# The beginning of a hybrid decoder step: tokens in halves, the first weight block loaded ahead of x, identity products on TensorE

## The chip, the core and the metric

The kernel runs on one core of one Trainium2 chip. The metric is the device time of one execution in microseconds, and a version's time is the median of its runs. In the profile PE is TensorE's products, PEld its weight loads, DVE the vector engine, ACT the scalar engine, POOL GpSimd, and SP the engine that issues most DMAs. A name with a q behind it (ACTq, SPq) is the engine's queue issuing a DMA.

## The reference, cut to what matters

One layer of a decoder trunk. All three head groups (NSA attention, RWKV-7, memory attention) read the same projection of the normalised tokens, 1024 of the prompt and 8 samples:

```python
h = rms_norm(x_prompt, ln_g)                 # x_prompt: 1 x 1024 x 1024
q, kv, g, z, u_rw, z_rw, q_mem, z_mem = split_in(h @ w_in)    # w_in: 1024 x 3480
# the same for x_sample (8 x 1 x 1024)
prev = concatenate([prev_row, u_rw[:-1]]); u = u_rw + (prev - u_rw) * mu
# then the recurrence on u, two kinds of attention, gates and the output projection
```

Only the start of this is touched by the change: the normalisation, h and the first columns of the projection, u_rw (896 columns from column 1816 on).

## The kernel before, in words

The prompt's 1024 tokens are worked in two halves H of 512 tokens, four tiles of 128 tokens each. For a product of near full precision each operand is split in a high part, rounded to fp32r, and a low part, the rest: three products (high x high, high x low, low x high) stand for one.

`load_x` (L171) loads four tiles x of 128 x 1024. `norm_x` (L180) squares each on ACT with a running sum (L186), makes the reciprocal root by nine small operations on DVE for each tile (`rsqrt`, L118: L125 to L136), and scales the tile in place on DVE (L188). `load_xs` does the same for the samples. `make_hTs` (L222) turns the samples' rows on TensorE (p_hs, L228), multiplies by the gains on DVE (hs, L231), and POOL writes the high and low parts into the last eight columns of each h tile (L235, L236). `make_hT` (L202) turns x on TensorE: for each of eight blocks k of 128 channels four transposes fill one PSUM tile p_h (L208); ACT writes the high part of h, 128 x 512 (L211), and DVE the low part (L212).

`w_load` (L241) loads a block of 128 columns of w_in on SP (wraw, two buffers), and `w_split` (L250) makes its high part on ACT (whi, L255) and its low part on DVE (wlo, L256), two buffers each. `project` (L259) multiplies one block with one half of the tokens: for H = 0 in two pieces of 256 and 264 columns, p_pr (L268), 24 products each; three PSUM tiles are there for p_pr. `u_half` (L530) runs over the seven blocks of u_rw, and `do_u` (L285) mixes each with the row before it on ACT (L294) and DVE (L301 to L307).

The order of the program: samples, four x tiles, two weight blocks, the other four x tiles (all these loads on SP but the samples' one), norm of the first half, hs, split of the two blocks, h of the first half, block 0 with its two pieces interleaved by k, blocks 1 to 6; the norm of the second half and its h are woven into these. A scheduler puts each engine's instructions into one fixed order from this; every engine works strictly in that order. `issue_after` holds a group back until an instruction named in it is placed. `rwkv_open` (L575) loads constants from ACT's queue.

Of the kernel before, what the change touches and what calls it, by code (L numbers as in the profile page):

```python
# [10 lines left out]
F32 = mybir.dt.float32  # L11
# [3 lines left out]
AF = mybir.ActivationFunctionType  # L15
OP = mybir.AluOpType
# [3 lines left out]
D = 1024  # L20
T = 1024
NS = 8
HALF = 512
# [24 lines left out]
def bc(ap, shape):  # L48
    return ap.to_broadcast(shape)
# [18 lines left out]
def group(gen, n):  # L68

    while list(islice(gen, n)):  # L70
        yield
# [42 lines left out]
class Step:  # L114
# [53 lines left out]
        return self.vec[:, k:k + n]  # L168


    def load_x(self, H):  # L171
        xs = []
        for t in range(4):
            x = self.xp.tile([128, D], F32, name="x", tag="x", bufs=8)
            r0 = H * HALF + t * 128
            self.nc.sync.dma_start(x[:], self.I["x_prompt"][0, r0:r0 + 128, :])
            xs.append(x)
        return xs

    def norm_x(self, xs):  # L180
        nc = self.nc
        self.xn = {}
        ss = self.small.tile([128, 4], F32, name="ss_x")
        for t in range(4):
            j = self.xp.tile([128, D], BF, name="sqx", tag="sqx", bufs=1)
            self.last_sq = nc.scalar.activation(j[:], xs[t][:], AF.Square, accum_out=ss[:, t:t + 1])  # L186
            r = self.rsqrt(self.small, ss[:, t:t + 1], 1, 1.0 / D, 1e-6)
            self.last_x = nc.vector.tensor_scalar(xs[t][:], xs[t][:], r, None, op0=OP.mult)  # L188
            self.xn[t] = xs[t]

    def load_xs(self):
        nc, I = self.nc, self.I
        x = self.xp.tile([128, D], F32, name="xs", tag="xs")
# [5 lines left out]
        nc.vector.tensor_scalar(x[:NS], x[:NS], r, None, op0=OP.mult)  # L199
        self.xsn = x  # L200

    def make_hT(self, H):  # L202

        nc = self.nc
        for k in range(8):
            ps = self.pw.tile([128, 512], F32, name="p_h", tag="w") if k % 2 and H == 0 else self.ptr.tile([128, 512], F32, name="p_h", tag="tr")
            for t in range(4):
                nc.tensor.transpose(ps[:, t * 128:(t + 1) * 128], self.xn[t][:, k * 128:(k + 1) * 128], self.ident[:])  # L208
            hi, lo = (x[k] for x in self.h8) if H == 0 else self.h_tiles(H, k)
            g = self.v("ln_g", k)  # L210
            nc.scalar.activation(hi[:, :HALF], ps[:], AF.Copy, scale=g)  # L211
            nc.vector.scalar_tensor_tensor(lo[:, :HALF], ps[:], g, hi[:, :HALF].bitcast(F32),  # L212
                                           op0=OP.mult, op1=OP.subtract)
            self.hi[H].append(hi)
            self.lo[H].append(lo)
            yield

    def h_tiles(self, H, k):
        W = HALF + (NS if H == 0 else 0)
# [1 line left out]

    def make_hTs(self):  # L222
        nc = self.nc
        self.h8 = list(zip(*(self.h_tiles(0, k) for k in range(8))))
        if True:
            ps = self.ptr.tile([128, 512], F32, name="p_hs", tag="tr")
            for k in range(8):
                nc.tensor.transpose(ps[:, k * NS:(k + 1) * NS], self.xsn[:NS, k * 128:(k + 1) * 128],  # L228
                                    self.ident[:NS, :NS])
# [17 lines left out]
        self.last_w = nc.sync.dma_start(raw[:, :, :n], src)  # L247
        return raw

    def w_split(self, raw, n):  # L250
# [4 lines left out]
        nc.scalar.activation(hi[:, :, :n], raw[:, :, :n], AF.Copy)  # L255
        nc.vector.tensor_tensor(lo[:, :, :n], raw[:, :, :n], hi[:, :, :n].bitcast(F32), op=OP.subtract)  # L256
        return hi, lo

    def project(self, H, hi, lo, m, out, first=False):  # L259

        pieces = ((0, 256), (256, 520)) if H == 0 else ((0, 512),)
        pss = [self.ppr.tile([128, 512], F32, name="p_pr", tag="pr") for _ in pieces]
        parts = [(ps, a, b, k) for ps, (a, b) in zip(pss, pieces) for k in range(8)]
        if first:
            parts.sort(key=lambda x: x[3])
        for n, (ps, a, b, k) in enumerate(parts):
            for i, (w, h) in enumerate(((hi, self.hi[H]), (hi, self.lo[H]), (lo, self.hi[H]))):
                self.last_mm = self.pe.matmul(ps[:m, :b - a], w[:, k, :m], h[k][:, a:b],  # L268
                                              start=(k == 0 and i == 0), stop=(k == 7 and i == 2))
# [143 lines left out]
    def phase1(self):  # L413
        tc, nc, I, O = self.tc, self.nc, self.I, self.O
# [7 lines left out]
        with ExitStack() as ctx:  # L422
# [18 lines left out]
            self.pe = self.te = nc.tensor  # L441
            with ExitStack() as xctx:
                self.xp = xctx.enter_context(tc.tile_pool(name="xp", bufs=1, reuse_waits="tile"))
                self.load_xs()
# [84 lines left out]

    def u_half(self, H):  # L530
        self.U = self.up.tile([128, 2, 7, 256], F32, name="U")
        for j in range(7):
            hi, lo = self.ready.pop(0) if self.ready else self.wblock(1816 + j * 128, 128)
            out = []
            yield from self.project(H, hi, lo, 128, out, (H, j) == (0, 0))
            self.do_u(H, out, j)

    def columns(self, tiles):
# [902 lines left out]
    def phase2(self):  # L1441
        tc, nc, I, O = self.tc, self.nc, self.I, self.O
        with ExitStack() as ctx:
# [23 lines left out]
            ready, spent = [0.0] * 4, [0.0] * 4  # L1467
            rate = START

# [363 lines left out]
    def sample_nsa(self):  # L1833
# [3 lines left out]
        with ExitStack() as ctx:  # L1837
# [15 lines left out]
            with P("snsx") as xp:  # L1853
# [479 lines left out]
```

## Time and profile before

| | |
|---|---|
| runs | 1008.6, 1008.91, 1014.28 us; median 1008.91 |
| the profiled execution | 1011.9 us |
| its span, first to last instruction | 1010.1 us, mean granted clock 0.981 |
| busy | PE 948.4 (94%), PEld 788.3 (78%), DVE 679.4 (67%), ACT 441.9 (44%), POOL 252.1 (25%) |
| PE in the first of 40 slices (25 us) | 5 tenths; 9 or more in 33 of the others, 8 or less in 6 |

The shares are means over stages of different kinds. For an edit at the start one reads the start: the timeline of the first microseconds, engine by engine, and, in square brackets, how long the engine sat idle before a row and what released it. A row of the timeline merges neighbours of one kind; the number behind the x says how many.

### The profile page before, as it was taken

Reading aid. Unit: us, or ns where it says so; the run is one execution under the profiler, and the core shown is the slowest. Engines: PE = TensorE matmul, PEld = TensorE weight load, DVE = VectorE, ACT = ScalarE, POOL = GpSimd, SP = SyncE. Lnnn points to the kernel's source line nnn. Section 1 sums busy time; section 2 is a strip of 40 time slices with the busy share of each in tenths; the row PEclk is TensorE's granted clock in tenths of the full one; section 3 lists DMA queues with packets and bytes.
Section 4 is the critical chain, followed back from the end, with each engine's and each line's share of the span. In section 5 each row is a group of like instructions: output and inputs, shape, how many; then the busy total and the mean of one; then the engine's idle time right before and its main releaser. Section 6 shows DMA issues by size and latency. Waiting matters only on the chain.

```text
span 1010.1 us, 24649 instructions
## 1 busy us (share of the span) xinstructions
PE 948.4 (94%) x9887; PEld 788.3 (78%) x9887; DVE 679.4 (67%) x1965; ACT 441.9 (44%) x987; POOL 252.1 (25%) x220
## 2 busy tenths in 40 slices
PE   5999999999999998999987999999999988999997
PEld 4999888778887877788866777887878876777964
DVE  7669489546773997543547677775779986457465
ACT  7554333223532432223425666656467655224312
POOL 1000000000000000000007765766578853112010
PEclk9999999899999999999996999999999999999999
DMA  8323114113230162256245323331210063995522
GB/s 280 105 64 89 41 53 116 54 44 85 72 106 3 50 176 65 59 135 156 66 148 177 101 64 100 132 87 39 50 38 17 27 148 100 297 290 185 153 78 76
DMA packets 133979, 104.20 MB, mean 103 GB/s; under 512 B 34594, under 2 KB 121129, under 8 KB 133737
## 3 DMA queue, kind: packets, MB, share of 16 engines
q1 hardware_dynamic: 128904, 90.92, 31.3%
q0 software_dynamic: 3200, 10.49, 3.1%
q8 instruction: 78, 1.28, 0.5%
q10 hardware_dynamic: 1760, 1.21, 0.4%
q14 instruction: 37, 0.30, 0.1%
HBM read 84.00 MB, written 22.78 MB: 106 GB/s over the span
## 4 chain that ended last, share of the span: by engine, by line
PE 35%; DVE 10%; ACT 6%; DMA 3%; issue 2%; SPq 2%; POOL 1%; ACTq 0%; DVEq 0%; POOLq 0%
PE p_s L86 5%; PE p_pT L86 5%; PE p_out L86 5%; PE p_pr L268 4%; PE p_o L86 4%; PE p_pr L86 2%; ACT p L1298 2%; DMA wor<-in_w_out_dram 2%; ACT p L1307 1%; PE p_hid L86 1%; DVE nm L1297 1%; PE p_sc L86 1%; SPq L1818 1%; DVE pt L1258 1%; POOL p L1312 1%
## 5 line engine op out<-in xcount | busy, mean ns | idle before, releaser
L86 PE MATMUL p_pr<-h,whi 128*128 128x512 f32 (+5 forms) x928 | 234.2, 344 | 2.3 <-issue 2.3
L1312 POOL TENSOR_SCALAR p<-p,fac 128x640 f32<-128x640 f32 (+7 forms) x128 | 211.2, 1665 | 93.8 <-DVE fac L1309 37.4
L86 PEld LDWEIGHTS p_pr<-h,whi 128*128 128x128 f32 (+1 forms) x928 | 149.3, 186 | 21.8 <-issue 5.3
L86 PE MATMUL p_pr<-h,wlo 128*128 128x512 f32 (+5 forms) x464 | 154.3, 332 | 0.0
L959 POOL MEMSET w2d<- 128x128 f32 x1 | 0.2, 205 | 388.5 <-PE p_it L86 388.5
L86 PEld LDWEIGHTS p_pr<-h,wlo 128*128 128x128 f32 (+1 forms) x464 | 86.3, 186 | 9.9
L268 PE MATMUL p_pr<-h,whi 128*128 128x256 f32 (+2 forms) x416 | 87.2, 306 | 0.4 <-ACT whi L255 0.2
L86 PE MATMUL p_pT<-ident,p 128*128 128x128 f32 x528 | 74.4, 285 | 5.1 <-ACT pt L1256 2.3
L86 PE MATMUL p_s<-kh,qs 128*128 128x512 f32 (+3 forms) x191 | 72.3, 386 | 4.5 <-ACT p L1298 4.5
L86 PEld LDWEIGHTS p_pT<-ident,p 128*128 128x128 f32 x528 | 58.7, 144 | 17.4 <-issue 7.1
L86 PE MATMUL p_o<-pt,vs 128*64 128x128 f32 x1056 | 70.0, 282 | 1.1 <-DVE c_r L1232 0.7
L1298 ACT ACTIVATE p<-p_s,nm 128x640 f32<-128x640 f32 (+3 forms) x64 | 55.7, 873 | 33.4 <-DVE nm L1297 27.5
L1297 DVE TENSOR_REDUCE nm<-p_s 128x1 f32<-128x640 f32 (+3 forms) x64 | 57.6, 918 | 17.4 <-PE p_s L86 17.3
L268 PEld LDWEIGHTS p_pr<-h,whi 128*128 128x128 f32 x416 | 66.3, 190 | 3.7 <-ACT whi L255 0.7
L256 DVE TENSOR_TENSOR wlo<-wraw,whi 128x1024 fp32r<-128x1024 f32 (+1 forms) x35 | 41.8, 1196 | 37.3 <-ACT whi L255 37.3
L86 PEld LDWEIGHTS p_o<-pt,vs 128*64 128x64 f32 x1056 | 59.0, 140 | 6.7 <-issue 2.7
L268 PE MATMUL p_pr<-h,wlo 128*128 128x256 f32 (+2 forms) x208 | 62.7, 303 | 0.2 <-DVE wlo L256 0.2
L86 PE MATMUL p_s<-kl,qs 128*128 128x512 f32 (+3 forms) x192 | 62.6, 342 | 0.0
L1258 DVE COPY pt<-p_pT 128x512 f32<-128x512 f32 (+1 forms) x72 | 48.0, 671 | 17.2 <-PE p_pT L86 16.7
L255 ACT ACTIVATE whi<-wraw 128x1024 fp32r<-128x1024 f32 (+1 forms) x35 | 36.3, 1038 | 51.5 <-PE p_pr L86 37.8
L1256 ACT ACTIVATE pt<-p_pT 128x512 f32<-128x512 f32 (+1 forms) x72 | 42.1, 588 | 30.6 <-PE p_pT L86 30.1
L86 PE MATMUL p_out<-woh,chi 128*128 128x512 f32 x128 | 52.3, 408 | 1.7 <-ACT woh L2154 1.6
(535 smaller groups left out, 1985.8 us busy)
## 6 DMA issues: line engine op xcount, KB each, us to landing
wraw<-in_w_in_dram SPq DMA_DIRECT2D x34, 512.0 KB
pg<-in_c_pool_dram SPq DMA_DIRECT2D x40, 256.0 KB
pg<-in_c_pool_dram SPq DMA_DIRECT2D x48, 128.0 KB
x<-in_x_prompt_dram SPq DMA_DIRECT2D x8, 512.0 KB
z_d<-zt SPq DMA_DIRECT2D x16, 256.0 KB
cat<-z_d SPq DMA_DIRECT2D x8, 512.0 KB
xres<-in_x_prompt_dram POOLq DMA_DIRECT2D x16, 256.0 KB, 3.9
wor<-in_w_out_dram SPq DMA_DIRECT2D x16, 256.0 KB
```

The lines of the kernel that those rows point to most:

```text
L86: self.last = getattr(self.engine, op)(*a, **k)
L255: nc.scalar.activation(hi[:, :, :n], raw[:, :, :n], AF.Copy)
L256: nc.vector.tensor_tensor(lo[:, :, :n], raw[:, :, :n], hi[:, :, :n].bitcast(F32), op=OP.subtract)
L268: self.last_mm = self.pe.matmul(ps[:m, :b - a], w[:, k, :m], h[k][:, a:b], start=(k == 0 and i == 0), stop=(k == 7 and i == 2))
L959: nc.gpsimd.memset(w2d[:], 0.0)
L1256: nc.scalar.activation(pt[:, :n], ps[:, :n], AF.Copy)
L1258: nc.vector.tensor_copy(pt[:, :n], ps[:, :n])
L1297: V.tensor_reduce(nm[:, h, b:b + 1], ps[:, c0:n1], axis=AX.X, op=OP.max, negate=True)
L1298: A.activation(Ps[h, b][:, :n1 - c0], ps[:, c0:n1], AF.Exp, bias=nm[:, h, b:b + 1], accum_out=sm[:, h, b:b + 1])
L1307: A.activation(Ps[h, b][:, :n1], ps[:, h, :n1], AF.Exp, bias=nm[:, h, b:b + 1], accum_out=sm[:, h, b:b + 1])
L1312: nc.gpsimd.tensor_scalar(x, x, f[:, h, b:b + 1], None, op0=OP.mult)
L1818: self.last_page = nc.sync.dma_start(dst[:, c], page[:, c0:c0 + 256])
```

## The change

Seven edits, all in the first phase:

- SP loads weight block 0 ahead of the four x tiles and block 1 behind them; ACT and DVE split block 0 before the first row sums.
- The norm goes by two tiles at a time: one reciprocal root of two columns in twelve steps for both. In the later two of four tiles, the last one's scale is done by ACT and no longer by DVE.
- h goes by halves of 256 tokens: a PSUM tile p_h now holds two k of 256 columns. ACT's and DVE's operations on it have 256 columns and are twice as many.
- Blocks 0 and 1 both do their first 256 tokens before either does its last 264.
- Block 1's low part is made on POOL.
- 34 products of the identity with itself (p_w, plain f32) stand first on TensorE; nothing reads them.
- The four squares of the second half's tiles are held until the last high part of the first half is placed.

The diff's core:

```diff
+WARM = 34
-    def norm_x(self, xs):
-        ss = self.small.tile([128, 4], F32, name="ss_x")
-        for t in range(4):
-            self.last_sq = nc.scalar.activation(j[:], xs[t][:], AF.Square, accum_out=ss[:, t:t + 1])
-            r = self.rsqrt(self.small, ss[:, t:t + 1], 1, 1.0 / D, 1e-6)
-            self.last_x = nc.vector.tensor_scalar(xs[t][:], xs[t][:], r, None, op0=OP.mult)
+    def square_x(self, xs):
+        ss = self.small.tile([128, 2], F32, name="ss_x")
+        for t, x in enumerate(xs):
+            self.last_sq = nc.scalar.activation(j[:], x[:], AF.Square, accum_out=ss[:, t:t + 1])
+        return ss
+    def norm_x(self, xs, t0, ss=None):
+        ss = ss or self.square_x(xs)
+        r = self.rsqrt(self.small, ss[:], 2, 1.0 / D, 1e-6)
+        for t, x in enumerate(xs):
+            if t and t0:
+                nc.scalar.activation(x[:], x[:], AF.Copy, scale=r[:, t:t + 1])
+            else:
+                self.last_x = nc.vector.tensor_scalar(x[:], x[:], r[:, t:t + 1], None, op0=OP.mult)
+    def warm(self):
+        ps = self.pw.tile([128, 512], F32, name="p_w", tag="w")
+        for n in range(WARM):
+            self.nc.tensor.matmul(ps[:, :128], self.ident[:], self.ident[:], start=True, stop=True)
...
+    def make_hT(self, H, half):
+        for k0 in range(0, 8, 2):
+            pool, tag = (self.pw, "w") if k0 % 4 and H == 0 else (self.ptr, "tr")
+            ps = pool.tile([128, 2, 256], F32, name="p_h", tag=tag)
+            for j in range(2):
+                for t in range(2):
+                    nc.tensor.transpose(ps[:, j, t * 128:(t + 1) * 128],
+                                        self.xn[2 * half + t][:, (k0 + j) * 128:(k0 + j + 1) * 128], self.ident[:])
+            for j in range(2):
...
+                self.last_hi = nc.scalar.activation(hi[:, c], ps[:, j], AF.Copy, scale=g)
+                self.last_lo = nc.vector.scalar_tensor_tensor(lo[:, c], ps[:, j], g, hi[:, c].bitcast(F32),
+                                                              op0=OP.mult, op1=OP.subtract)
...
-                self.load_xs()
-                xs0 = self.load_x(0)
-                raws = [self.w_load(1816 + j * 128, 128) for j in range(2)]
-                xs1 = self.load_x(1)
-                self.norm_x(xs0)
-                self.make_hTs()
-                with tc.issue_after(self.last_x.ins):
-                    self.ready = [self.w_split(raw, 128) for raw in raws]
-                for _ in self.make_hT(0):
-                    pass
+                self.warm()
+                self.load_xs()
+                raws = [self.w_load(1816, 128)]
+                xs0 = self.load_x(0, range(4))
+                raws.append(self.w_load(1816 + 128, 128))
+                xs1 = self.load_x(1, range(4))
+                self.ready = [self.w_split(raws[0], 128)]
+                self.norm_x(xs0[:2], 0)
+                scaled = self.last_x.ins
+                self.norm_x(xs0[2:], 2)
+                self.ready.append(self.w_split(raws[1], 128, G))
+                with tc.issue_after(scaled):
+                    self.make_hTs()
+                first = self.u_half(0)
+                with tc.issue_after(self.last_sq.ins):
+                    for half in range(2):
+                        for _ in self.make_hT(0, half):
+                            pass
+                        for _ in range(4):
+                            next(first)
                 with tc.issue_after(self.last_sq.ins):
                     self.rwkv_open()
-                first = self.u_half(0)
-                for _ in range(8):
+                for _ in range(16):
                     next(first)
-                self.norm_x(xs1)
-                for _ in weave(group(first, 8), self.make_hT(1)):
+                with tc.issue_after(self.last_hi.ins):
+                    sss = [self.square_x(xs1[t:t + 2]) for t in (0, 2)]
+                for t in (0, 2):
+                    self.norm_x(xs1[t:t + 2], t, sss[t // 2])
+                for _ in weave(group(first, 8), chain(self.make_hT(1, 0), self.make_hT(1, 1))):
                     pass
...
     def u_half(self, H):
+        begun = [[], []] if H == 0 else []
+        for pieces in ((0, 256),), ((256, 520),):
+            for j, out in enumerate(begun):
+                hi, lo = self.ready[j]
+                for n, _ in enumerate(self.project(H, hi, lo, 128, out, pieces)):
+                    yield
+                if len(out) == 2:
+                    self.do_u(H, out, j)
```

What this does to the fixed orders is not plain from the diff. In the rows below a row of the new program has the line numbers of the new file. First TensorE from its first product on; p_hs are the samples' transposes, p_h those of x, p_pr the projection. Before:

```order
L228 MATMUL p_hs<-ident,xs 128x8 x8
L208 MATMUL p_h<-ident,x 128x128 x20
L268 MATMUL p_pr<-h_0_219,whi 128x256
L268 MATMUL p_pr<-h_0_219,whi 128x264
L268 MATMUL p_pr<-h_0_219,whi 128x256
L208 MATMUL p_h<-ident,x 128x128 x4
L268 MATMUL p_pr<-h_0_220,whi 128x256
L268 MATMUL p_pr<-h_0_219,wlo 128x256
```

And in the change:

```order
L203 MATMUL p_w<-ident 128x128 x34
L246 MATMUL p_hs<-ident,xs 128x8 x8
L223 MATMUL p_h<-ident,x 128x128 x16
L284 MATMUL p_pr<-h_0_243,whi 128x256 x2
L284 MATMUL p_pr<-h_0_244,whi 128x256
L284 MATMUL p_pr<-h_0_243,wlo 128x256
L284 MATMUL p_pr<-h_0_244,whi 128x256
L284 MATMUL p_pr<-h_1_245,whi 128x256
L223 MATMUL p_h<-ident,x 128x128 x4
L284 MATMUL p_pr<-h_1_246,whi 128x256
```

The 34 products stand ahead of everything, the samples' transposes too. The 16 transposes are those of the first two x tiles; the next four, of the other two tiles, stand between products of k = 0 and k = 1. From about the 410th row on TensorE's order is the same in both programs.

Second, ACT from the samples' square on. Before:

```order
L197 ACTIVATE sqx,ss_s<-xs 8x1024
L186 ACTIVATE sqx,ss_x<-x 128x1024 x4
L255 ACTIVATE whi<-wraw 128x1024 x2
L579 DMA c_rw<-in_c_rw_dram 128x480
L586 DMA wa_328<-in_rwkv_w_dram 64x256
L587 DMA wa_328<-in_rwkv_a_dram 64x256
L601 DMA lnw<-in_rwkv_ln_w_dram 128x256
L601 DMA lnw<-in_rwkv_ln_b_dram 128x256
L211 ACTIVATE h_0_219<-p_h,vec 128x512
```

And in the change:

```order
L211 ACTIVATE sqx,ss_s<-xs 8x1024
L273 ACTIVATE whi<-wraw 128x1024
L186 ACTIVATE sqx,ss_x<-x 128x1024 x4
L619 DMA c_rw<-in_c_rw_dram 128x480
L273 ACTIVATE whi<-wraw 128x1024
L626 DMA wa_411<-in_rwkv_w_dram 64x256
L232 ACTIVATE h_0_243<-p_h,vec 128x256
```

Block 0's split has come to the front; block 1's still stands ahead of the first part of h, and three of the five DMA issues have gone behind that part.

Third, ACT again, a little later: the last parts of h of the first 256 tokens, the issues, and a part of the next 256 tokens (h_7 to h_3).

```order
L232 ACTIVATE h_7_257<-p_h,vec 128x256
L627 DMA wa_411<-in_rwkv_a_dram 64x256
L641 DMA lnw<-in_rwkv_ln_w_dram 128x256
L641 DMA lnw<-in_rwkv_ln_b_dram 128x256
L232 ACTIVATE h_3_249<-p_h,vec 128x256
```

The three issues stand between the two halves of the first half's h. Seven rows on, behind the last part of h of the next 256 tokens, the change has the later squares:

```order
L232 ACTIVATE h_7_257<-p_h,vec 128x256
L186 ACTIVATE sqx,ss_x<-x 128x1024
L659 ACTIVATE rk<-U,vec 128x256
L310 ACTIVATE U<-p_pr,dv 128x256
L186 ACTIVATE sqx,ss_x<-x 128x1024
L659 ACTIVATE rk<-U,vec 128x256
L186 ACTIVATE sqx,ss_x<-x 128x1024
L310 ACTIVATE U<-p_pr,dv 128x256
L273 ACTIVATE whi<-wraw 128x1024
```

Before, the same place reads so:

```order
L211 ACTIVATE h_5_229<-p_h,vec 128x512
L186 ACTIVATE sqx,ss_x<-x 128x1024
L211 ACTIVATE h_4_227<-p_h,vec 128x512
L211 ACTIVATE h_7_233<-p_h,vec 128x512
L211 ACTIVATE h_6_231<-p_h,vec 128x512
L186 ACTIVATE sqx,ss_x<-x 128x1024 x3
L159 DMA gains<-in_nsa_q_norm_dram 128x64
L294 ACTIVATE U<-p_pr,dv 128x256 x2
L255 ACTIVATE whi<-wraw 128x1024
```

The squares of the later tiles and block 2's split (the last whi in both) have moved behind all 16 parts of the first half's h. Much later, at some 70 rows of SP's queue, a few loads of constants have changed places by about ten rows.

More of the change, by code (lines that the diff above doesn't have):

```diff
@@ L168, in v, with load_x @@
         return self.vec[:, k:k + n]
-    def load_x(self, H):
+    def load_x(self, H, tiles):
         xs = []
-        for t in range(4):
+        for t in tiles:
             x = self.xp.tile([128, D], F32, name="x", tag="x", bufs=8)
@@ L178, in load_x @@
         return xs
[L180 removed]
+    def square_x(self, xs):
         nc = self.nc
[L182 to L184 removed]
+        ss = self.small.tile([128, 2], F32, name="ss_x")
+        for t, x in enumerate(xs):
             j = self.xp.tile([128, D], BF, name="sqx", tag="sqx", bufs=1)
[L186 to L189 removed]
+            self.last_sq = nc.scalar.activation(j[:], x[:], AF.Square, accum_out=ss[:, t:t + 1])
+        return ss
+    def norm_x(self, xs, t0, ss=None):
+        nc = self.nc
+        ss = ss or self.square_x(xs)
[5 more added lines that the diff above has]
+                self.last_x = nc.vector.tensor_scalar(x[:], x[:], r[:, t:t + 1], None, op0=OP.mult)
+            self.xn[t0 + t] = x
+    def warm(self):
+        ps = self.pw.tile([128, 512], F32, name="p_w", tag="w")
+        for n in range(WARM):
+            self.nc.tensor.matmul(ps[:, :128], self.ident[:], self.ident[:], start=True, stop=True)
     def load_xs(self):
         nc, I = self.nc, self.I
[L193 removed]
+        x = self.xsn = self.xp.tile([128, D], F32, name="xs", tag="xs")
         nc.scalar.dma_start(x[:NS], I["x_sample"][:, 0, :])
@@ L199, in load_xs @@
         nc.vector.tensor_scalar(x[:NS], x[:NS], r, None, op0=OP.mult)
-        self.xsn = x
-    def make_hT(self, H):
+    def make_hT(self, H, half):
         nc = self.nc
[L205 to L216, printed above, removed]
+        for k0 in range(0, 8, 2):
[6 more added lines that the diff above has]
+            for j in range(2):
+                k = k0 + j
+                if len(self.hi[H]) <= k:
+                    for x, y in zip((self.hi[H], self.lo[H]), (y[k] for y in self.h8) if H == 0 else self.h_tiles(H, k)):
+                        x.append(y)
+                g, c = self.v("ln_g", k), slice(half * 256, half * 256 + 256)
+                hi, lo = self.hi[H][k], self.lo[H][k]
+                self.last_hi = nc.scalar.activation(hi[:, c], ps[:, j], AF.Copy, scale=g)
+                self.last_lo = nc.vector.scalar_tensor_tensor(lo[:, c], ps[:, j], g, hi[:, c].bitcast(F32),
+                                                              op0=OP.mult, op1=OP.subtract)
+                yield
     def h_tiles(self, H, k):
@@ L223, in make_hTs @@
         nc = self.nc
-        self.h8 = list(zip(*(self.h_tiles(0, k) for k in range(8))))
         if True:
@@ L248, in w_load, with w_split @@
         return raw
-    def w_split(self, raw, n):
+    def w_split(self, raw, n, low=None):
         nc = self.nc
@@ L255, in w_split, with project @@
         nc.scalar.activation(hi[:, :, :n], raw[:, :, :n], AF.Copy)
-        nc.vector.tensor_tensor(lo[:, :, :n], raw[:, :, :n], hi[:, :, :n].bitcast(F32), op=OP.subtract)
+        (low or nc.vector).tensor_tensor(lo[:, :, :n], raw[:, :, :n], hi[:, :, :n].bitcast(F32), op=OP.subtract)
         return hi, lo
-    def project(self, H, hi, lo, m, out, first=False):
-        pieces = ((0, 256), (256, 520)) if H == 0 else ((0, 512),)
+    def project(self, H, hi, lo, m, out, pieces=None):
+        pieces = pieces or (((0, 256), (256, 520)) if H == 0 else ((0, 512),))
         pss = [self.ppr.tile([128, 512], F32, name="p_pr", tag="pr") for _ in pieces]
         parts = [(ps, a, b, k) for ps, (a, b) in zip(pss, pieces) for k in range(8)]
-        if first:
-            parts.sort(key=lambda x: x[3])
         for n, (ps, a, b, k) in enumerate(parts):
@@ L443, in phase1 @@
                 self.xp = xctx.enter_context(tc.tile_pool(name="xp", bufs=1, reuse_waits="tile"))
+                G = nc.gpsimd
+                self.xn = {}
+                self.warm()
                 self.load_xs()
-                xs0 = self.load_x(0)
-                raws = [self.w_load(1816 + j * 128, 128) for j in range(2)]
-                xs1 = self.load_x(1)
-                self.norm_x(xs0)
-                self.make_hTs()
-                with tc.issue_after(self.last_x.ins):
-                    self.ready = [self.w_split(raw, 128) for raw in raws]
-                for _ in self.make_hT(0):
-                    pass
+                raws = [self.w_load(1816, 128)]
[7 more added lines that the diff above has]
+                self.ready.append(self.w_split(raws[1], 128, G))
+                self.h8 = list(zip(*(self.h_tiles(0, k) for k in range(8))))
+                with tc.issue_after(scaled):
[7 more added lines that the diff above has]
+                            next(first)
                 with tc.issue_after(self.last_sq.ins):
                     self.rwkv_open()
-                first = self.u_half(0)
-                for _ in range(8):
+                for _ in range(16):
                     next(first)
-                self.norm_x(xs1)
-                for _ in weave(group(first, 8), self.make_hT(1)):
+                self.xn = {}
+                with tc.issue_after(self.last_hi.ins):
[3 more added lines that the diff above has]
+                for _ in weave(group(first, 8), chain(self.make_hT(1, 0), self.make_hT(1, 1))):
                     pass
@@ L531, in u_half @@
         self.U = self.up.tile([128, 2, 7, 256], F32, name="U")
-        for j in range(7):
-            hi, lo = self.ready.pop(0) if self.ready else self.wblock(1816 + j * 128, 128)
+        begun = [[], []] if H == 0 else []
[3 more added lines that the diff above has]
+                for n, _ in enumerate(self.project(H, hi, lo, 128, out, pieces)):
+                    yield
+                if len(out) == 2:
+                    self.do_u(H, out, j)
+        for j in range(len(begun), 7):
+            hi, lo = self.wblock(1816 + j * 128, 128)
             out = []
-            yield from self.project(H, hi, lo, 128, out, (H, j) == (0, 0))
+            yield from self.project(H, hi, lo, 128, out)
             self.do_u(H, out, j)
```

## The prediction

> **What bounds the kernel now.** I read the busy times by stretch first, for the stage in which the change lies. Columns: length, then busy us and instruction count of PE, PEld, DVE, ACT and POOL, PEclk, DMA share, GB/s.
>
> ```profile
> 0.00:10.82 10.82, 1.01 (x8) 0.92 (x9) 5.22 (x35) 6.83 (x10) 3.08 (x17) 1.00 0.84 274
> 10.82:18.27 7.45, 6.28 (x23) 4.43 (x23) 7.34 (x27) 4.51 (x8) 1.86 (x8) 1.00 1.05 379
> 18.27:30.85 12.58, 12.58 (x106) 12.58 (x107) 12.20 (x55) 9.60 (x18) 0.00 (x0) 1.00 0.44 116
> 30.85:64.00 33.15, 32.99 (x278) 32.75 (x277) 18.26 (x52) 16.54 (x28) 0.00 (x0) 1.00 0.40 107
> ```
>
> From 18.27 on TensorE hardly pauses: 12.58 us of 12.58, then 32.99 of 33.15. Only what lies before 18.27 is to be had, and whatever is late at 30.85 stays late, since behind the second half's transposes the order on TensorE is the same in both programs. Next, TensorE's timeline up to there.
>
> ```profile
> 7.92 1.01 PE L228 MATMUL p_hs<-ident,xs 8*128 8x8 f32 x8 [7.92 <-DVE xs L199]
> 10.82 2.70 PE L208 MATMUL p_h<-ident,x 128*128 128x128 f32 x10 [1.88 <-DVE x L188]
> 14.04 2.63 PE L208 MATMUL p_h<-ident,x 128*128 128x128 f32 x10 [0.52 <-DVE x L188]
> 16.82 0.99 PE L268 MATMUL p_pr<-h,whi 128*128 128x256 f32 x3
> 18.27 0.66 PE L208 MATMUL p_h<-ident,x 128*128 128x128 f32 x4 [0.47 <-DVE h L212]
> ```
>
> It waits for scaled rows of x, then for the low parts of h (L212). Behind these waits stand, on ACT and DVE:
>
> ```profile
> 6.56 1.06 ACT L186 ACTIVATE sqx<-x 128x1024 bf16<-128x1024 f32 x1
> 8.59 1.06 ACT L186 ACTIVATE sqx<-x 128x1024 bf16<-128x1024 f32 x1 [0.88 <-DMA x<-in_x_prompt_dram]
> 11.63 1.06 ACT L255 ACTIVATE whi<-wraw 128x1024 fp32r<-128x1024 f32 x1 [0.61 <-DMA wraw<-in_w_in_dram]
> 13.34 1.06 ACT L255 ACTIVATE whi<-wraw 128x1024 fp32r<-128x1024 f32 x1 [0.66 <-DMA wraw<-in_w_in_dram]
> 14.54 0.75 DVE L188 TENSOR_SCALAR x<-x,rq_r 128x1024 f32<-128x1024 f32 x1
> 15.20 2.35 DVE L256 TENSOR_TENSOR wlo<-wraw,whi 128x1024 fp32r<-128x1024 f32 x2
> 14.30 0.61 ACTq L587 DMA_DIRECT2D wa<-in_rwkv_a_dram  x1
> 14.95 0.60 ACTq L601 DMA_DIRECT2D lnw<-in_rwkv_ln_w_dram  x1
> 15.59 0.44 ACTq L601 DMA_DIRECT2D lnw<-in_rwkv_ln_b_dram  x1
> 16.08 3.00 ACT L211 ACTIVATE h<-p_h,vec 128x512 fp32r<-128x512 f32 x5 [1.68 <-PE p_h L208]
> 17.47 2.72 DVE L212 SCALAR_TENSOR_TENSOR h<-p_h,vec,h 128x512 fp32r<-128x512 f32 x4
> ```
>
> Three things are to be seen. Loads set the pace up to 13.34 (x2 at 8.59, the two weight blocks at 11.63 and 13.34). DVE then does the fourth scale, both weight differences and the low parts in one row without a gap from 14.54. And ACT's first h comes right behind its last DMA issue (15.59 + 0.44 = 16.03): an issue holds ACT's queue.
>
> **The change, part by part.** *Loads.* From x2's landing to the second block's are three transfers in 13.34 - 8.59 = 4.75 us, 1.6 each. The first block ahead of x puts each x 1.6 to 1.75 later: x1, there by 6.56, lands at about 8.3, x3 at about 11.2. The second block keeps its place behind the same six transfers: 13.34. Bounds: half a transfer each way.
>
> *First half's scale.* Square of x1 8.3 + 1.24 = 9.55. The rsqrt for two columns is 12 steps; a chain of such steps on eight columns runs from 89.58 to 91.46 in ten gaps, 0.19 each:
>
> ```profile
> 89.58 0.16 DVE L126 TENSOR_SCALAR rq_g<-rq_a 128x8 int32<-128x8 int32 x1
> 91.46 0.17 DVE L136 SCALAR_TENSOR_TENSOR rq_r<-rq_t,rq_r 128x8 f32<-128x8 f32 x1
> ```
>
> 12 x 0.19 = 2.3, to 11.85, and two scales of 0.75 overlapping a little, to 13.25. The first block's difference (1.22) now runs in DVE's pause near 6.5 and costs nothing; if the block were late it would push this chain.
>
> *Identity products.* They need the identity matrix alone, whose load is the first on SP as vec's is on ACT; vec had landed at 2.77. Each product is two records, as in p_pc, where 8 products are these 16 records:
>
> ```profile
> 2.77 0.17 DVE L593 TENSOR_SCALAR dv<-vec 128x7 f32<-128x7 f32 x1 [2.77 <-DMA vec<-in_c_vec_dram]
> 451.21 1.91 PE L941 MATMUL p_pc<-w1s,peT 128*2 128x128 f32 x16
> 10.82 1.33 PE L208 MATMUL p_h<-ident,x 128*128 128x128 f32 x5 [1.88 <-DVE x L188]
> L208 PE MATMUL p_h<-ident,x x64: 270/273/476, 10.8 to 66.1; 128*128 128x128 f32 x64
> ```
>
> Taking off the last record's drain (a lone one takes 0.273), a record is 0.11 and a product 0.22. But at 10.82 five transposes took 1.33, without a slow drain of 0.476 0.21 each; at 18.27 four took 0.66, 0.13 each. The early pace is about half, though PEclk says 1.00 for both. At the slow pace a product is 0.43. The pace changed between 17.4 and 18.27, 0.6 to 7.4 us after TensorE had begun to work (10.82) or to multiply (16.82). So after the start at 2.9 it changes between 3.5 and 10.3, and 34 products end between 10.6 and 14.0. I take the change at 8, a little past the middle since p_h's transposes needed nearly the 7.4: 12 x 0.43 + 22 x 0.22, ending at 12.8.
>
> [...]
>
> Behind them are p_hs (8 in about 0.9, to 13.7), though x is scaled at 13.25, and then 16 transposes x 0.11, to 15.45. First product at 15.45 (16.82 before), but these earlier steps run at the full pace.
>
> *First half of h.* Copies and differences of 256 columns go by the U rows of that shape:
>
> ```profile
> 25.17 0.46 ACT L294 ACTIVATE U<-p_pr,dv 128x256 f32<-128x256 f32 x1
> 25.52 0.46 ACT L294 ACTIVATE U<-p_pr,dv 128x256 f32<-128x256 f32 x1
> 26.61 0.48 DVE L301 SCALAR_TENSOR_TENSOR U<-p_pr,vec,U 128x255 f32<-128x255 f32 x1
> 27.00 0.15 DVE L127 TENSOR_SCALAR rq_a<-rq_a 128x1 f32<-128x1 f32 x1
> ```
>
> ACT 0.35 apart, DVE 0.4. ACT is free at 13.34 + 1.06 = 14.4. DVE must do hs (waits for p_hs, 13.9), the second rsqrt (to 15.8), eight differences (3.2) and x2's scale (0.66) and is done at about 20; TensorE, in order behind it, ends block 0's first half at 20.85.
>
> *Second half.* Three ACT issues (0.61 + 0.60 + 0.44 = 1.65, some 0.3 of it under the copy before) stand ahead of the second copies, which begin at 20.85. TensorE has 11 transposes, a short wait, then block 1's first half (24 x 0.12), to 24.8, and both second halves (48 x 0.12 = 5.75; the third stretch above has 106 records in 12.58): the two blocks end at 30.55. Before: 30.85. Gain 0.3.
>
> *Behind it.* Block 2's split needs block 0's buffer, now free only at the end of its second half (27.8), and ACT has the four squares of the later tokens in one place:
>
> ```profile
> 24.11 1.06 ACT L186 ACTIVATE sqx<-x 128x1024 bf16<-128x1024 f32 x1
> 25.07 0.19 ACT L186 ACTIVATION_READ_ACCUMULATOR sqx<-x 128x1 f32 x1
> 30.85 0.60 PE L208 MATMUL p_h<-ident,x 128*128 128x128 f32 x4
> 32.42 0.39 PE L268 MATMUL p_pr<-h,wlo 128*128 128x256 f32 x1 [0.16 <-DVE wlo L256]
> 35.21 0.28 PE L268 MATMUL p_pr<-h,whi 128*128 128x264 f32 x1
> ```
>
> ACT from 20.85: eight short operations (2.9), square (1.25), two short (0.8), square: 27.0. DVE: rsqrt 2.3, U 0.7, scale 0.66, difference 1.22: 31.95. TensorE is there at 30.55 + 4 x 0.12 + 2 x 0.11 = 31.25 and waits 0.8 with the overlaps. Before, 30.85 to 35.21 is 4.36 us for 7 transposes and 26 products, 0.77 + 3.1 of work, so 0.5 of waiting. Loss 0.3.
>
> *POOL and SP.* Block 1's low part goes to POOL. The same subtraction takes 0.741 there for 256 columns, so at most 3.0 for 1024. It can begin at 14.4 and stands behind nine small operations on hs; TensorE asks for it at 22.2: nothing. On SP block 2's load finds its buffer free earlier, which nobody uses before 27.8. Far behind, some constant loads go ten places down SP's queue; the first of them to be used, w2d, is wanted at 486.0: nothing.
>
> ```profile
> L1188 POOL TENSOR_TENSOR qhl<-q,qhl 128x256 fp32r<-128x256 f32 x15 | 11.0, 741 | 67.4 <-ACT qhl L1187 67.4
> L1188 DVE TENSOR_TENSOR qhl<-q,qhl x9: 403/417/1008, 695.6 to 815.6; 128x256 fp32r<-128x256 f32 x9
> 693.70 3.75 POOL L1312 TENSOR_SCALAR p<-p,fac 128x640 f32<-128x640 f32 x2 [1.80 <-DVE fac L1309]
> 695.63 1.01 DVE L1188 TENSOR_TENSOR qhl<-q,qhl 128x256 fp32r<-128x256 f32 x1 [1.23 <-ACT qhl L1187]
> L988 PE MATMUL p_co<-w2d,phid x2: 275/312/348, 486.0 to 486.2; 128*128 128x128 f32 x2
> ```
>
> *Sum.* -0.3 + 0.3 = 0. The profiled execution took 1011.9 (span 1010.1), 3.0 over the median 1008.9, so 1008.9 for the runs. Unknown costs: the products' end (10.6 to 14.0) moves the sum by -0.6 to +1.1, the landings by -0.3 to +0.4, the ACT issues by -0.3 to 0. Own range 1007.5 to 1010.5.
>
> **Rivals.** *The chains on ACT and DVE keep up.* Then TensorE is dense from a first product at 14.9: 96 products x 0.12 and 16 transposes end at 28.2, 2.65 before 30.85: 1006.2. For it: DVE was busy 12.20 of 12.58 us before without stopping TensorE. Against: every chain above leaves DVE no slack until 20.
>
> *The slow pace stays until real products come.* Then 34 x 0.43 = 14.6 from 2.9: 17.4 instead of 12.8, and hs, the rsqrt and the low parts, which queue on DVE behind p_hs, are all 4.7 later: 1013.6, slower. It decides when the change of pace comes after about 10. For it: 20 transposes did not change it before. Against: the products are not transposes.
>
> *POOL and DVE hold each other up.* DVE's own 128x256 subtraction took 1008 ns once instead of 417, at 695.63, with POOL's long operation from 693.70 under way. With three DVE operations (two rsqrt steps, x2's scale) inside POOL's long one, 3 x 0.6 = 1.8, of which 0.3 is won back in later waits: 1010.4. It decides if the long one is still running at 17.2, when x2's scale is due. [...]
>
> **How the numbers follow.** Forecast 0.5, first rival 0.27, slow pace 0.1, POOL 0.13. Time: 1008.9. For 8 in 10 the range takes in the first rival with the low end of its unknowns (1005) and most of the slow pace (1013). About 1% (10 us) is what a measurement tells from no change. Faster by that needs nearly all of the 11.0 us that TensorE stands idle before 18.27 (18.27 - 1.01 - 6.28), and for most of them x is not there: 0.01. Slower needs over twice the slow-pace rival: 0.02. Within: 0.97.
>
> **What would show it.** Right: p_w ends between 12 and 14, first p_pr near 15.4 with gaps of 0.5 to 1 behind it, block 0's first half ends near 20.8, the second blocks end near 30.5, and block 2 waits about 0.8 for wlo on DVE. Wrong: p_w past 15 (slow pace); no gap between the first product and 28 (first rival); x2's scale much over 0.75 with POOL's wlo beside it; or a time 3 us off with the start as computed, which would put the cause behind 64 us.

## The result, and the profile after

The change runs in 1002.93 us (median of 13 runs, 998.95 to 1006.0) against 1008.6 for the kernel before in the same session: ratio 0.994, 95% interval 0.9917 to 0.9964. I had forecast 1008.9 with 1005 to 1013. So 5.7 us were won where I saw none, and the time lies below my range. The profiled execution took 1003.45 (span 1001.1). A run over 1.5% above the fastest of its kernel is left out of the ratios; in all that follows it is one, of 1019.53 us, in the experiment e3.

The stages of the start first, with the columns and borders used for the kernel before:

```profile
0.00:10.82 10.82, 8.01 (x56) 8.01 (x57) 4.55 (x21) 6.64 (x9) 1.52 (x9) 1.00 0.85 286
10.82:18.27 7.45, 5.48 (x45) 4.54 (x43) 6.93 (x25) 4.58 (x10) 4.22 (x14) 1.00 1.06 390
18.27:30.85 12.58, 11.55 (x84) 11.47 (x85) 8.60 (x28) 9.87 (x21) 1.03 (x4) 0.86 0.31 85
30.85:64.00 33.15, 33.15 (x277) 32.93 (x277) 20.58 (x72) 17.30 (x31) 0.00 (x0) 1.00 0.41 112
```

The third row, full before, is no longer so: 11.55 of 12.58, at a granted clock of 0.86. TensorE's timeline shows where the start went:

```profile
2.81 9.59 PE L203 MATMUL p_w<-ident 128*128 128x128 f32 x68 [2.81 <-DMA ident<-in_c_mat_dram]
12.33 0.66 PE L246 MATMUL p_hs<-ident,xs 8*128 8x8 f32 x8
13.00 2.30 PE L223 MATMUL p_h<-ident,x 128*128 128x128 f32 x16
15.06 0.48 PE L284 MATMUL p_pr<-h,whi 128*128 128x256 f32 x2
19.30 0.73 PE L223 MATMUL p_h<-ident,x 128*128 128x128 f32 x4 [2.50 <-DVE x L197]
33.60 0.64 PE L284 MATMUL p_pr<-h,whi 128*128 128x256 f32 x4
```

Up to 15.06 it goes nearly as computed. Then TensorE waits 2.50 us for x, and block 2's first products (the last row), which tell the end of the first two blocks, start at 33.60; before, the two blocks end at 30.85. The change's start is slower, and yet the kernel is faster.

To find the gain I split the program at the first and the last product of one tile, p_at (the recurrence), which every version runs in the same order. The row gives the least, median and greatest duration in ns, then the first and the last start. Before:

```profile
L86 PE MATMUL p_at<-ident,ar x16: 270/272/332, 100.6 to 376.5; 128*128 128x128 f32 x16
```

After:

```profile
L87 PE MATMUL p_at<-ident,ar x16: 270/272/331, 104.4 to 373.0; 128*128 128x128 f32 x16
```

Up to the first: 3.8 us lost. From the first to the last: 275.9 before, 268.6 after, 7.3 won. From the last to the span's end: 633.6 and 628.1, 5.5 won. In both parts the order of the products on TensorE is the same in all sixteen traces of this document (3750 and 5461 records).

What is in the middle? TensorE's waits on "issue", in the table of waits before (total, times, longest). The rows are those of the whole execution; all these waits end between 190 and 400 us.

```profile
PE p_pr L86 <- issue: 2.3, 1, 2.3
PE p_it L86 <- issue: 2.0, 2, 1.5
PE p_iy L86 <- issue: 1.3, 2, 1.0
```

and after:

```profile
PE p_r L87 <- issue: 0.8, 1, 0.8
PE p_iy L87 <- issue: 0.6, 1, 0.6
PE p_it L87 <- issue: 0.6, 2, 0.4
PE p_pr L87 <- issue: 0.3, 1, 0.3
```

"issue" means that TensorE waited for nothing that the profile shows. These waits come to 5.67 us before and 2.35 after, 4.11 and 1.24 of it between the two p_at. The biggest one before, and the granted clock (the third number from the end in the second fence) in the 3.41 us from just before its end and in the 6.83 after those:

```profile
304.77 0.80 PE L86 MATMUL p_pr<-h,whi 128*128 128x256 f32 x2 [2.33 <-issue]
```

```profile
304.37:307.78 3.41, 3.01 (x20) 2.77 (x24) 0.00 (x0) 0.39 (x1) 0.00 (x0) 0.50 0.03 5
307.78:314.61 6.83, 6.83 (x292) 6.12 (x293) 1.70 (x4) 1.61 (x5) 0.00 (x0) 1.00 0.02 5
```

A wait of 2.33 us, and behind it a window of 3.41 us at half the clock. Between the two p_at the kernel before has 10.24 us of such windows, the change none. At half the clock they cost at most 5.1 us, and the waits cost 2.9 more: enough for the 7.3. With the waits and half of the windows taken off, the middle lasts 266.6 to 268.7 us in all sixteen traces.

What TensorE waits for there shows when its recorded instructions (weight loads and semaphore instructions too) are counted up to each such wait:

```
before: 4289 5057 7105 9409 9665        after: 4545 5057 7361 9665 10433
```

All ten are 193 more than a multiple of 256. The profile's table of queues (transfers, MB) before:

```profile
q8 instruction: 78, 1.28, 0.5%
```

That is 78 transfers of 16.4 KB for TensorE's 20,016 recorded instructions, one for each 256.6. From these counts I take it that TensorE's program arrives in blocks of 256 instructions, and that the waits stand at the borders of blocks. The 34 products are 136 instructions; at the first p_at the change has 139 more behind it than the kernel before. By that, every border moves to another place of the same program. I call that the refill theory. For 78 transfers the trace shows 5 such waits, and one of the five is 2.33 us long.

### The profile page after: what moved, and what is told of

The parts are those of the page before. It is cut to its first block, busy times and chain, and to the rows that moved or that the text cites. A ratio compares the mean times of both kernels' runs of the same rounds, so it can differ in the third digit from the quotient of the medians.

```text
span 1001.1 us, 24786 instructions
## 1 busy us (share of the span) xinstructions
PE 948.8 (95%) x9955; PEld 788.9 (79%) x9955; DVE 681.4 (68%) x1954; ACT 446.8 (45%) x1005; POOL 254.0 (25%) x221
## 4 chain that ended last, share of the span: by engine, by line
PE 65%; DVE 18%; ACT 6%; issue 4%; DMA 3%; POOL 2%; SPq 2%; ACTq 0%; DVEq 0%; POOLq 0%
PE p_pr L87 20%; PE p_pr L284 8%; PE p_out L87 5%; PE p_s L87 4%; PE p_pT L87 4%; PE p_o L87 3%; ACT p L1338 2%; POOL p L1352 2%; PE p_iy L87 2%; DVE nm L1337 1%; PE p_hid L87 1%; PE p_z L87 1%; PE p_it L87 1%; ACT p L1347 1%; DVE pt L1298 1%
## 5 line engine op out<-in xcount | busy, mean ns | idle before, releaser
L87 PE MATMUL p_pr<-h,whi 128*128 128x512 f32 (+5 forms) x928 | 231.0, 340 | 0.3 <-issue 0.3
```

Of the source, the lines that this page charges most:

```text
L87: self.last = getattr(self.engine, op)(*a, **k)
```

## The experiments

The rivals: the clock theory (the products bring the full pace early), the start theory (halves and load order), and chance (half-pace windows fall where they may). The runs of the kernel before beside the experiments had medians of 1008.38, 1009.27, 1012.24 and 1009.04 in the four sessions, each on another chip, so I compare ratios to those.

The table has for each kernel: the instructions put ahead beyond those of the kernel before, as its trace counts them at the first p_at; the ratio; then from the same trace the first p_at, the time from the first to the last p_at, the rest to the end, and the sum of the "issue" waits of the whole execution, all in us. A product is four instructions; a few semaphore instructions more or less come to that. Each trace is of one run: e8's is the slowest of its seven (1003.93), those of e4, e6, e9, e10 and e13 are the fastest of theirs.

```
                                   ahead  ratio  95% interval      p_at    to last   rest   waits
before, first trace                    0                            100.6   275.9   633.6   5.67
after                                139  0.994  0.9917 to 0.9964   104.4   268.6   628.1   2.35
e1  before, again                      0  1.0016 0.9987 to 1.0045   100.2   273.6   632.9   4.25
e2  before + 34 products             135  0.9981 0.9959 to 1.0003   105.3   269.2   630.2   2.10
e3  change, no products                4  0.9999 0.9973 to 1.0025   102.5   274.6   628.9   4.58
e4  change, 64 narrow products       259  1.0194 1.0161 to 1.0227   120.6   272.5   630.0   3.38
e5  before + 34 tiny                 135  0.9951 0.9930 to 0.9972   101.5   268.6   632.9   1.78
e6  before + 16 tiny                  63  0.9969 0.9944 to 0.9993   102.2   269.5   625.6   1.00
e7  before + 50 tiny                 199  0.9992 0.9968 to 1.0015   101.8   270.7   631.1   4.07
e8  change, low part on DVE          142  0.9904 0.9877 to 0.9931   100.4   270.8   630.8   3.20
e9  e8 with 16 wide products          70  0.9967 0.9938 to 0.9996   100.8   269.5   630.9   3.22
e10 e8 with 34 tiny                  142  0.9908 0.9876 to 0.9939   100.9   269.9   626.7   3.38
e11 before + 64 tiny                 255  0.9993 0.9970 to 1.0016   102.3   275.1   631.6   4.77
e12 e8 with 33 products              138  0.9928 0.9904 to 0.9952   100.5   269.0   630.5   2.13
e13 e8 with 35 products              146  0.9931 0.9909 to 0.9954   101.3   269.9   626.1   2.45
e14 before + 35 tiny                 139  0.9948 0.9929 to 0.9967   102.3   269.3   629.6   2.45
```

**Where do the waits come from (e1 to e4).** e1 is the kernel before. e2 adds to it the products alone:

```diff
+                self.warm()
                 self.load_xs()
```

e3 takes that line out of the change. e4 keeps it with more and narrower products:

```diff
-WARM = 34
+WARM = 64
-            self.nc.tensor.matmul(ps[:, :128], self.ident[:], self.ident[:], start=True, stop=True)
+            self.nc.tensor.matmul(ps[:, :32], self.ident[:], self.ident[:, :32], start=True, stop=True)
```

> The kernel before, unchanged, for the granted clock of many of its runs and a second trace. Refill theory (TensorE's instructions come in blocks of 256, and the change, which puts 139 more of them ahead, moves the block borders against the program): the trace again shows TensorE idle for no visible reason at the same places of the program, some 1.5 us near 193 and 2.3 us near 304, with a half-pace window behind each; time 1008.6. Chance theory (the half-pace windows fall where they happen to fall): the windows stand at other places in this trace, and the mean clock of the runs scatters from 0.98 to 0.99 as widely as that of the change.

> The kernel before with the 34 identity products alone put in front; nothing else of the change. Refill theory: the 136 more instructions move the block borders nearly as the change does, so the unexplained waits near 193 and 304 go and some 5 to 8 us are won behind 66 us: 1001 to 1004, with the start a little better or worse. Clock theory (the gain is that the products set the clock's windows off earlier): about the same time, 1001 to 1004. Start theory (the gain comes from tokens in halves and the order of loads): 1007 to 1010, no gain.

> The change without its identity products; all else of it stays. Refill theory: only 3 instructions more than before stand ahead, so the block borders lie as before, the waits near 193 and 304 come back, and the time is 1007 to 1011. Clock theory: no early products, the pace changes late as before: 1007 to 1011 too. Start theory: the gain stays, 1001 to 1004.

> The change with 64 identity products of 32 columns in place of 34 of 128: about as long on TensorE, but 259 instructions more than before, which is 3 more than one block of 256. Refill theory: the block borders lie against the program as in the kernel before, so the waits near 193 and 304 come back and the gain is lost: 1006 to 1011. Clock theory: TensorE is at work as early as in the change, the gain stays: 1001 to 1004. Start theory: the gain stays too.

In e1 and e3 both long waits are back at the old places of the program (1.19 and 2.32 in e1, 1.53 and 2.15 in e3), in e4 the longest (2.44); in e2 they are gone (0.61 and 0.20 are the nearest). From the first p_at to the last it takes 272.5 to 275.9 with 0, 4 or 259 instructions ahead, and 269.2 with 135. That speaks for the refill theory there and against the others. Chance alone does not place the half-pace windows either: in e1 the two behind the long waits stand where they stood (194.9 and 304.1 for 195.1 and 304.4), and four later ones stand 3.7 us earlier (822.9 for 826.6, for one) in a program that is 2.7 earlier at its last p_at. Only the window at 413.6, and e1's at 450.9 and 993.6, have no counterpart. But in time e2's 0.2% is not clear of no gain, since its start is 4.7 us later (first p_at 105.3 for 100.6). And e4 missed its 1006 to 1011 by far, at 1027.25, for its products took 27.5 us and put the start 20 us off:

```profile
2.90 27.52 PE L203 MATMUL p_w<-ident 128*128 128x32 f32 x128 [2.90 <-DMA ident<-in_c_mat_dram]
```

That is 0.215 us a record to the end: 32 columns a product never brought the full pace, which products of 128 or 256 columns brought after 3.2 to 5.7 us in six traces (3.7 in the change's). The 16 transposes of x right behind them took 3.55 us, as in e3 without products (3.70); in the change they took 2.30.

**The shift without the products (e5 to e7, e11).** In the kernel before, products of 8 rows and columns, over in 1.85 us:

```diff
+            self.nc.tensor.matmul(ps[:8, :8], self.ident[:8, :8], self.ident[:8, :8], start=True, stop=True)
```

> The kernel before with 34 identity products of 8 rows and 8 columns in front: 136 instructions more, as with the 34 full ones, but over by about 7 us, before the first transposes, and too little work to change TensorE's pace. Refill theory: the waits near 193 and 304 go, waits stand only where the instruction's number is 193 modulo 256, the start is as before, and the whole gain shows: 1000 to 1003. Clock theory: no gain, 1008. Start theory: no gain, 1008.

> The kernel before with 16 such tiny products: 64 instructions more, a quarter of a block. Refill theory: the borders lie at new places; which groups they cut is not worked out beforehand, so the time can lie anywhere from 1000 to 1009, but each unexplained wait of over 0.2 us again has a number of 193 modulo 256, and the wait of 2.3 us at the old place near 304 is changed. Clock theory and start theory: 1008.

> The kernel before with 50 such tiny products: 200 instructions more, over by about 9.2 us. Refill theory: as for 16, anywhere from 1000 to 1009 with waits at 193 modulo 256 alone. Clock theory and start theory: 1008.

> The kernel before with 64 tiny products in front: 256 instructions more, one whole block, so the borders lie as in the kernel before. Refill theory: the waits near 193 and 304 are back, at instruction numbers 256 higher, and the time is that of the kernel before plus some 1 to 4 us, since the products are over only at about 11 us: 1008.5 to 1012. If any products in front help: 1003 to 1006 as with 16 and 34.

34 tiny products, which compute nothing and leave TensorE at its slow pace (the first six transposes of x behind them took 1.89 us, in e2 five behind the full products took 0.83), won 0.49%, 1004.59 for 1009.27, a little less than I expected since its start is 0.9 later. 16 and 50 of them (e6 and e7) have waits of 1.00 and 4.07 us and 0.9969 and 0.9992. 64 of them, one block exactly, won nothing (0.9993), and brought the waits back:

```profile
195.18 0.34 PE L87 MATMUL p_it<-iY,iT 32*32 32x32 f32 x18 [1.75 <-issue]
306.00 0.40 PE L87 MATMUL p_pr<-h,whi 128*128 128x256 f32 x2 [2.62 <-issue]
```

So it is not the number of products that helps but where the borders fall. The change's number was luck: 63, 70 and 199 instructions ahead also bring the middle to 269.5 to 270.7, so it is the kernel before whose borders fall badly there. The same stretch of 10 us around that place, in the kernel before, in e5 and in e11:

```profile
300.00:310.00 10.00, 7.67 (x232) 6.91 (x232) 1.32 (x3) 1.54 (x4) 0.00 (x0) 0.83 0.28 79
```

```profile
300.00:310.00 10.00, 10.00 (x318) 8.50 (x319) 1.75 (x4) 2.37 (x7) 0.00 (x0) 1.00 0.02 7
```

```profile
300.00:310.00 10.00, 7.38 (x230) 6.85 (x230) 1.48 (x4) 1.56 (x5) 0.00 (x0) 0.83 0.29 82
```

TensorE's records in it (the number behind its busy time) go from 232 to 318 and back to 230, its clock from 0.83 to 1.00 and back. All five traces with the wait of over 2 us there have the half-pace window behind it, none of the other eleven has one at that place. In all traces together there are 66 such waits on "issue", and 64 stand at 193 modulo 256. Each of these 64 ends 1.2 to 1.6 us after the latest transfer of the instruction queue has landed, and 2.2 to 2.9 after that transfer began. The two others, 0.15 and 0.28, stand at p_k, over 6 us after a landing. What starts a block's transfer the runs do not show.

**POOL and DVE (e8).** The change's DVE and POOL around its wait of 2.50:

```profile
15.34 2.34 POOL L274 TENSOR_TENSOR wlo<-wraw,whi 128x1024 fp32r<-128x1024 f32 x1
15.38 0.48 DVE L233 SCALAR_TENSOR_TENSOR h<-p_h,vec,h 128x256 fp32r<-128x256 f32 x1
15.77 1.93 DVE L136 TENSOR_TENSOR rq_t<-rq_t,rq_a 128x2 f32<-128x2 f32 x1
18.50 0.74 DVE L197 TENSOR_SCALAR x<-x,rq_r 128x1024 f32<-128x1024 f32 x1
```

A step on two columns, 0.16 elsewhere, ends at 17.70, just as POOL's subtraction does (17.68). So it does in e3 (1.95 long, to 17.41 for 17.39) and in e4 (1.62, to 35.40 for 35.39). x is scaled late by it, TensorE waits, and a half-pace window follows (granted clock 0.50):

```profile
20.11:23.53 3.42, 3.42 (x19) 3.42 (x18) 2.06 (x5) 1.27 (x4) 0.00 (x0) 0.50 0.51 146
```

e8 puts block 1's low part back on DVE:

```diff
-                self.ready.append(self.w_split(raws[1], 128, G))
+                self.ready.append(self.w_split(raws[1], 128))
```

> The change with block 1's low part back on DVE; all else stays, the number of instructions ahead too. In the change's trace a DVE step of 0.16 us lasts 1.93 beside POOL's subtraction of 2.34, TensorE then waits 2.5, and a half-pace window follows at 20.1. If POOL holds DVE up and the pause brings the window: the 1.93 becomes 0.16, DVE has 1.2 more to do itself, the window at 20.1 goes, and the time is 1 to 3 below the change's 1002.9: 1000 to 1002. If DVE's queue is the limit either way: the same 1003 or 1 more, the pause at another row.

998.96 us, 0.9904 of the kernel before; I had expected 1000 to 1002. Its DVE now, and TensorE ahead of the second transposes and at block 2:

```profile
13.64 1.22 DVE L274 TENSOR_TENSOR wlo<-wraw,whi 128x1024 fp32r<-128x1024 f32 x1
14.78 0.15 DVE L136 TENSOR_TENSOR rq_t<-rq_t,rq_a 128x2 f32<-128x2 f32 x1
18.34 0.75 DVE L197 TENSOR_SCALAR x<-x,rq_r 128x1024 f32<-128x1024 f32 x1
```

```profile
19.34 0.60 PE L223 MATMUL p_h<-ident,x 128*128 128x128 f32 x4
29.29 0.64 PE L284 MATMUL p_pr<-h,whi 128*128 128x256 f32 x4
30.22 0.39 PE L284 MATMUL p_pr<-h,wlo 128*128 128x256 f32 x1 [0.28 <-DVE wlo L274]
```

The step takes 0.15, no window follows, and block 2 starts at 29.29 for 33.60. The first p_at comes at 100.4, 4.0 earlier than in the change and 0.2 earlier than before. So POOL's part, with all that hangs on it, costs the change 4.0 us. How much of that is the held step, e8 does not show, for its edit changed the fixed orders too. On DVE seven low parts (three in the change) stand ahead of x's scale, and on TensorE 28 products (6 in the change) ahead of the transposes that need it. So x is scaled at 18.34, hardly earlier than the change's 18.50, and TensorE does not wait for it because it has other products until then. In the change's own order the held step is 1.8 us of the wait of 2.50 by the difference of 1.93 and 0.16, and the window costs at most 1.7; both are estimates. e3 has the same held step, but its pause is 1.33 us, no window follows, and its first p_at comes at 102.5, for the change's 104.4.

**What the products' work is worth, and a better version (e9, e10).** Both start from e8. e9 has 16 products of the identity with itself twice over, 256 columns; e10 the tiny ones:

```diff
-WARM = 34
+WARM = 16
+            self.nc.tensor.matmul(ps[:, :256].rearrange("p (a b) -> p a b", b=128), self.ident[:],
+                                  bc(self.ident[:, None, :], [128, 2, 128]), start=True, stop=True)
```

> The change with block 1's low part on DVE and 16 identity products of 256 columns in place of 34 of 128: about the same array work ahead, but 64 instructions of it and not 136 (67 more than before in all, as the kernel before with 16 tiny products has 64). Refill theory: waits for instructions come to about 0.5 us in all, as there (0.39 and 0.15), in place of 2.7; with the half-pace windows behind them 2 to 3 us less than the 999.0 of the version with the low part on DVE: 996 to 998. Chance or clock theory: no change from 999.

> The change with block 1's low part on DVE and the 34 identity products cut to 8 rows and columns: the same number of instructions, next to no array work. Refill theory: behind 80 us nothing changes, so the difference from 999.0 is what the early full pace of the clock is worth at the start: by my sum between -0.6 and +1.1, so 998.5 to 1000.5. Clock theory (the gain is the early pace): the gain is lost, 1004 to 1008.

e10 has the ratio of e8, 0.9908 and 0.9904. Its 1002.8 lies outside the range I gave in us because the kernel before took 1012.24 beside it. Its first p_at comes at 100.9 for 100.4, so the array's early work is worth some 0.5 us, and the versions with full products spread as much (100.4 to 101.3 in e8, e12 and e13). The clock theory falls. e9 was to be the best, and is not: 0.9967. I had carried e6's waits over to it, 63 instructions ahead for 70, and found a new one:

```profile
381.29 0.37 PE L87 MATMUL p_it<-iY,iT 32*32 32x32 f32 x18 [1.60 <-issue]
```

Seven instructions and another start were enough. Its waits come to 3.22, and e6's to 1.00.

**Does the exact border make up the rest (e12 to e14)?** e8 won 0.96%, e5 0.49%, with nearly the same borders. So 33 and 35 full products in e8, and 35 tiny ones in the kernel before.

> The version with the low part on DVE, with 33 full products in place of 34: 4 instructions fewer, 135 more than before in place of 139. If the exact place of the borders explains why this arrangement gains some 4 us more behind 80 us than the kernel before with 34 tiny products (136 more): the ratio to the kernel before rises from 0.990 to about 0.994. If it is the new arrangement of the start itself: 0.990 stays.

> The same with 35 products: 143 more instructions than before. If the gain hangs on the place of the borders to within a few instructions, the ratio lies anywhere from 0.990 to 0.997; if it is the arrangement: 0.990.

> The kernel before with 35 tiny products: 140 instructions more, within one of the change's 139. If the exact place of the borders is all: the ratio is near that of the change's low part on DVE, 0.990 to 0.992 (the start costs about 1.2 us, 0.001). If the arrangement wins the other 4 us: 0.995 as with 34.

0.9928, 0.9931 and 0.9948. Four instructions either way do not matter much, and the kernel before stays at 0.995 with 139 as with 135. The new start thus wins 0.2 to 0.5% beside the shift; 0.02 to 0.2% of it is the start itself (first p_at at 100.4 to 101.3 for 101.5 and 102.3). The rest, some 2 us on the mean, must lie behind the last p_at, since the middle takes no less (269.0 to 270.8 for 268.6 and 269.3). There single traces take 625.6 to 633.6 in no order that borders explain. They go, loosely, with the half-pace windows there, which come to 8.7 us (e10) to 36.0 (e5): around 510 to 575 the change, e10 and e13 have at most one, the others 7 to 20 us of them (e8: granted clock 0.87 from 511.4 to 575). This is not chance in single traces alone. The median granted clock of the runs is 0.990 or 0.991 in the change, e8, e10 and e13 and 0.988 in e3, for 0.983 to 0.987 in every kernel with the old start; but it is 0.986 in e12, 0.985 in e4 and 0.983 in e9. Many of these windows stand behind pauses of TensorE that every trace has. A wait of 2.14 to 2.42 us for DVE's pcq, at 538 to 560, has one behind it in twelve traces, and none in the change, e9, e10 and e13. A wait of 2.2 for ACT's p, at 812 to 836, has one in all sixteen. Why the same pause has the window behind it in one run and not in another, and why the new start more often has fewer, stays open.

## Why the prediction was wrong

- **The step that failed**: "whatever is late at 30.85 stays late, since behind the second half's transposes the order on TensorE is the same in both programs." The order is the same, the place in the instruction stream is not. 139 instructions more ahead of it win about 5 us between the first p_at and the last (268.6 to 270.8 with 135 to 146 ahead, 272.5 to 275.9 with 0, 4, 255 or 259). I had priced the products by their time alone, and put all that comes behind 64 us at nothing. The "issue" rows in the waits of before, 5.67 us with one of 2.3, were there to be read.
- **The start**: forecast 0, measured 3.8 later. Landings, products (2.81 to 12.40, forecast 2.9 to 12.8), transposes and first product (15.06, forecast 15.45) were right. The rival with POOL and DVE, to which I gave 0.13 and 1.5 us, was what happened, at up to 4.0: DVE was held once, for 1.93 us and to the end of POOL's operation, and I had left out the half-pace window behind the pause. Without it (e8) the sum comes out, -0.2 for 0, but in part by luck: e8's orders are not the change's, its two blocks end at 29.29, between my first rival's 28.2 and the forecast's 30.55, and what they win is given back by the first p_at.
- **The slow pace**: it ended at 6.5, not at 8: 3.7 us from the first product; over six traces it is 3.2 to 5.7. With e4's narrow products it stayed for all of their 27.5 us, as the rival has it for full ones. But the early work is worth some 0.5 us (e8 and e10), within my bounds.
- **Sum**: 3.8 lost at the start (4.0 better in e8), 5.0 to 7.3 won by the borders in the middle (268.6 for 273.6 and 275.9), and so 2 to 4.5 behind it. There the trace before has 27.3 us at half the clock and the change's 15.0, enough for up to 6.1 us; why, the runs don't settle.

## What to carry to other kernels

Instructions added at the front of this long unrolled program moved the waits on "issue" behind them, and with 34 tiny products (e5) the time changed by half a per cent (0.9951), here for the better by luck. Read the waits on "issue" first, and test a change that adds instructions against the same number of empty ones. An operation priced at nothing on an idle POOL can cost DVE beside it: here POOL's subtraction of 2.34 us held a DVE step of 0.16 for 1.93. And an edit that moves one operation can change every engine's fixed order: read the orders of both versions before the difference is put down to the operation.

## What was not expected of the hardware

- TensorE's waits for instructions, up to 2.62 us, at 193 modulo 256, in and behind groups of 64 products of 32 x 32 (p_it and p_iy).
- A DVE step of 0.16 us on two columns held for 1.93 us, to the end of POOL's subtraction of 2.34, while the operation just before it, which reads p_h, kept its 0.48.
- Pauses of 2.1 to 2.6 us with a half-pace window of 3.41 us behind them, but not behind each: the five waits for instructions over 2 us have one, and the 2.50 for x; of the sixteen waits for pcq twelve have.
- Products of 32 columns that kept the slow pace for 27.5 us.
